# Weights in one flat DRAM tensor in load order, and modulation on TensorE with four row tiles per load

## The chip, the cores and the metric

The kernel runs on one core of a Trainium2 chip. A core has a matrix engine (TensorE, PE in the profile; PEld is its weight load), VectorE (DVE), ScalarE (ACT), GpSimd (POOL) and a sync engine (SP) that issues the DMA transfers here. The metric is the device time of one execution in microseconds, lower is better; several runs are taken and the median counts. One of the executions is profiled, and all rows below come from it.

## The reference

One layer of an encoder over 256 tokens of width 2048, batch 1, all in float32. A conditioning vector c gives a shift, a scale and a gate for each of two sub-layers (adaLN modulation); one input projection feeds eight retention heads and eight latent-attention (MLA) heads; an output projection, a SwiGLU and a final norm follow.

```python
c_act = silu(c)
mod = (c_act @ ada_w + ada_b)                     # 2048 -> 6 x 2048
shift_a, scale_a, gate_a, shift_f, scale_f, gate_f = split(mod, 6)
h = rmsnorm(x, norm1_w) * (1 + scale_a) + shift_a
proj = h @ w_in                                   # 2048 -> 5184
q_r, k_r, v_r, g_r, cq, ckv, k_rope = split(proj)
ret_out = silu(g_r) * groupnorm(retention(rope(q_r), rope(k_r), v_r))
q_m = rmsnorm(cq) @ w_uq;  kv = rmsnorm(ckv) @ w_ukv
mla_out = rmsnorm(softmax_attention(q_m, kv, rope(k_rope)))
x = x + gate_a * (concat(ret_out, mla_out) @ w_o)
h = rmsnorm(x, norm2_w) * (1 + scale_f) + shift_f
x = x + gate_f * ((silu(h @ w_gate) * (h @ w_up)) @ w_down)     # 2048 -> 5632 -> 2048
return rmsnorm(x, final_norm_w)
```

Weights are read once: some 312 MB in one execution, a third of it ada_w.

## The kernel before

Weights arrive in loads of mostly 512 KB into one of six staging buffers `stg` (128 partitions of 1024 floats). A load of a projection weight covers two row tiles of 128 rows and 512 columns: in the DRAM matrix that is, per partition, two pieces of 2 KB, one from each row tile. `split_weights` (line 97) issues it from SP (line 101), ACT rounds it to `whi` (line 103), DVE makes the remainder `wlo` (line 105), each with three buffers. PE multiplies in three products, activation-high by whi, activation-high by wlo, activation-low by whi (lines 111 to 113), in one-pass float32r, for two token blocks; a load of 512 columns thus feeds 12 matmuls.

The modulation is a matrix-vector product. `ada_set` (line 153) makes it for one of six sections and `nk` column tiles of 128, so `n` = 128 nk columns, from loads of `kk` row tiles (line 155: two where nk is 4, four where it is 2). A set goes to DVE or to PE, by strings of 0 and 1 (lines 41, 43, 55) and, for the first gate_f set, a fixed choice. On DVE each row tile is one multiply-add into `ada_acc` (line 179). On PE each row tile is one plain float32 matmul (line 175) with 32 columns of stationary operand (`c_pad`, one of them not zero) and the n weight columns streaming. Row tile k goes to partitions 32 (k mod 4) of a PSUM bank, that is to one of four column strips of 32 columns of the array:

```python
q = 32 * (k % 4)
PE.matmul(a[q:q + 32, 0:n], lhsT=c_pad[:, k], rhs=w[:, j], start=k < 4, stop=k >= KT - 4)
```

`finish` and `spread` then sum the strips and bring the result into `mod`, `gate_a` or `gate_f`.

There are ten sets on PE: two of 256 columns at the start, one more of 256 columns at about 200 us, and seven of 512 columns, eight loads each.

The order of the program is a list of steps. `run` (line 131) walks it and starts the loads of later steps as long as at most LOOK = 3 are ahead and it does not stand at a step of URGENT. `ada_stream` cuts the modulation into units of one load, which are spread among the projection steps, so that PE, DVE and the DMA queue are all used. A scheduler then sets each engine's final order. Each engine works through its own order, and waits there for semaphores; a load can be issued when the last reader of its buffer, mostly DVE, is done.

In time: the first modulation and the norm of x (to 26 us), the input projection in four groups of row tiles with the next group's modulation between (to some 240 us), the latent projections and attention, the retention heads with the output projection and gate_a, shift_f and scale_f (to 533 us), SwiGLU and down projection (to the end).

Of the kernel before, what the change touches and what calls it, by code (L numbers as in the profile page):

```python
# [8 lines left out]
F32 = mybir.dt.float32  # L9
# [47 lines left out]
URGENT = ("finish", "spread", "build_h2", "build_h1")  # L57
# [3 lines left out]

@with_exitstack
def encoder_block(ctx: ExitStack, tc: tile.TileContext, x, cols, rows, pos, ada_w, w_in, w_uq, w_ukv, w_o,
                  w_gate, w_up, w_down, out):
# [64 lines left out]
    # ---- steps: ("w", source, body) takes split weights, ("a", load, body) a loaded tile, ("f", body, name) nothing;  # L129
    # no loads are started ahead at the URGENT ones ----  # L130
# [175 lines left out]
    def project(gi, name, c0, widths):  # L306
# [3 lines left out]
        def body(kp, whi, wlo):  # L310
# [22 lines left out]
            ("w", w_in[(k0 + kp) * P:(k0 + min(kp + 2, nk)) * P, c0:c0 + sum(widths)], lambda hi, lo, kp=kp: body(kp, hi, lo))  # L333
# [92 lines left out]
    def up_q(hf):  # L426
# [31 lines left out]
        ws = [("w", w_uq[k * P:(k + 1) * P, hf * 768:(hf + 1) * 768], lambda hi, lo, k=k: body(k, hi, lo)) for k in range(4)]  # L458
# [511 lines left out]
```

## Time and profile before

| | before |
|---|---|
| median of 3 runs | 1287.1 us |
| lowest and highest | 1284.15 and 1289.62 us |
| span of the profiled execution | 1284.4 us |
| PE busy | 1241.4 us (97%) |
| DVE busy | 844.6 us (66%) |
| ACT busy | 599.6 us (47%) |
| DMA queue, share of 16 engines | 75.1% |
| HBM read | 312.11 MB, mean rate 245 GB/s with the writes |

The profile gives no time of the profiled execution but its span, from the first to the last instruction; it lies inside the range of the three runs, 2.7 us under their median. A row of a view in order of time gives start, duration, engine, line, operation, the tile written and the tiles read. Matmuls are pipelined, so how long PE needs for one is read from start to start, not from its duration. DMA share is the part of the time in which the 16 DMA engines have a packet under way; it can exceed 1 where packets overlap.

### The profile page before, as it was taken

How to read it: one execution, taken by the hardware profiler on the slowest of the kernel's cores; microseconds unless marked ns; L12 is line 12 of the kernel's file. 1: busy time of each engine (PE TensorE's matmuls, PEld its weight loads, DVE VectorE, ACT ScalarE, POOL GpSimd, SP SyncE). 2: the span in 40 equal slices, each digit the busy share in tenths (PEclk: the TensorE clock that was granted, in tenths of full speed). 3: DMA queues.
4: the chain of work that ended last, by engine and by line, in shares of the span. 5: the costliest groups of instructions: out<-in, count | busy, mean ns of one | idle time of the engine just before them, and what ended most of it. 6: DMA issues, size and time to landing. Idle time of an engine off the chain costs nothing.

```text
span 1284.4 us, 15784 instructions
## 1 busy us (share of the span) xinstructions
PE 1241.4 (97%) x5798; PEld 967.1 (75%) x5798; DVE 844.6 (66%) x1185; ACT 599.6 (47%) x811; POOL 1.7 (0%) x9
## 2 busy tenths in 40 slices
PE   5999999999999999899999999999999999999997
PEld 1576657678776688578888888888888888888885
DVE  2596788779997699797556546554754454545544
ACT  3553445555546565556444344444444443434443
POOL 0000000000000000000000000000000000000000
PEclk8999999999999999999999999999999999999999
DMA  9898898887887789798777767775876655565562
GB/s 315 304 298 297 263 315 290 291 293 255 303 258 262 264 290 316 255 336 299 217 225 217 225 191 252 233 213 167 279 230 198 221 189 192 196 196 193 190 193 97
DMA packets 166621, 315.24 MB, mean 245 GB/s; under 512 B 10248, under 2 KB 22664, under 8 KB 166032
## 3 DMA queue, kind: packets, MB, share of 16 engines
q1 hardware_dynamic: 166544, 314.24, 75.1%
q8 instruction: 45, 0.74, 0.2%
q14 instruction: 32, 0.26, 0.1%
HBM read 312.11 MB, written 2.10 MB: 245 GB/s over the span
## 4 chain that ended last, share of the span: by engine, by line
PE 82%; DVE 8%; DMA 5%; ACT 2%; issue 2%; SPq 0%; ACTq 0%; DVEq 0%
PE bank L112 24%; PE bank L113 24%; PE bank L111 23%; PE bank L175 4%; DVE wlo L105 3%; DVE ada_acc L179 2%; PE bank L127 2%; DMA stg<-in_ada_w 2%; DMA stg<-in_w_in 1%; DMA stg<-in_w_o 1%; ACT whi L103 1%; PE bank L491 1%; PE bank L490 1%; PE bank L515 1%; PE bank L592 1%
## 5 line engine op out<-in xcount | busy, mean ns | idle before, releaser
L105 DVE TENSOR_TENSOR wlo<-stg,whi 128x1024 fp32r<-128x1024 f32 (+2 forms) x400 | 478.7, 1199 | 343.4 <-ACT whi L103 336.5
L103 ACT CAST whi<-stg 128x1024 fp32r<-128x1024 f32 (+2 forms) x400 | 412.7, 1033 | 534.2 <-PE bank L113 418.6
L111 PE MATMUL bank<-whi,actt 128*128 128x512 f32 (+1 forms) x1184 | 457.4, 392 | 9.9 <-ACT whi L103 6.4
L112 PE MATMUL bank<-wlo,actt 128*128 128x512 f32 (+1 forms) x1184 | 460.2, 389 | 6.9 <-DVE wlo L105 6.1
L113 PE MATMUL bank<-whi,actt 128*128 128x512 f32 (+1 forms) x1184 | 457.9, 387 | 0.7 <-DVE actt L124 0.7
L111 PEld LDWEIGHTS bank<-whi,actt 128*128 128x128 f32 x1184 | 221.7, 188 | 69.5 <-ACT whi L103 13.1
L112 PEld LDWEIGHTS bank<-wlo,actt 128*128 128x128 f32 x1184 | 223.3, 189 | 63.6 <-DVE wlo L105 16.3
L113 PEld LDWEIGHTS bank<-whi,actt 128*128 128x128 f32 x1184 | 222.9, 188 | 45.2 <-DVE actt L124 1.4
L179 DVE SCALAR_TENSOR_TENSOR ada_acc<-stg,c_act,ada_acc 128x512 f32<-128x512 f32 (+1 forms) x240 | 175.0, 730 | 18.0 <-DMA stg<-in_ada_w 15.0
L111 PE MATMUL bank<-whi,ap 128*128 128x512 f32 x352 | 137.0, 389 | 0.0
L113 PE MATMUL bank<-whi,ap 128*128 128x512 f32 x352 | 136.9, 389 | 0.0
L112 PE MATMUL bank<-wlo,ap 128*128 128x512 f32 x352 | 136.9, 389 | 0.0
L175 PE MATMUL bank<-stg,c_pad 128*32 128x512 f32 (+1 forms) x320 | 67.3, 584 | 14.7 <-DMA stg<-in_ada_w 14.7
L111 PEld LDWEIGHTS bank<-whi,ap 128*128 128x128 f32 x352 | 66.1, 188 | 13.8
L113 PEld LDWEIGHTS bank<-whi,ap 128*128 128x128 f32 x352 | 66.1, 188 | 13.8
L112 PEld LDWEIGHTS bank<-wlo,ap 128*128 128x128 f32 x352 | 66.1, 188 | 13.5
L175 PEld LDWEIGHTS bank<-stg,c_pad 128*32 128x32 f32 x320 | 10.2, 114 | 38.3 <-issue 27.3
L205 DVE TENSOR_REDUCE mod<-bank 128x4 f32<-128x512 f32 (+3 forms) x18 | 8.0, 443 | 15.6 <-PE bank L201 15.6
L829 ACT ACTIVATE sgs<-bank 128x512 f32<-128x512 f32 x22 | 13.1, 597 | 10.5 <-PE bank L113 9.9
L124 DVE TENSOR_TENSOR actt<-hfull,actt 128x256 fp32r<-128x256 f32 x40 | 16.3, 418 | 1.3 <-ACT actt L123 1.3
L831 DVE TENSOR_TENSOR sgs<-bank,sgs 128x512 f32<-128x512 f32 x22 | 14.3, 682 | 0.6 <-PE bank L113 0.6
L811 DVE TENSOR_TENSOR ap<-bank,ap 128x512 fp32r<-128x512 f32 x22 | 14.1, 681 | 0.0
(222 smaller groups left out, 712.3 us busy)
## 6 DMA issues: line engine op xcount, KB each, us to landing
stg<-in_ada_w SPq DMA_DIRECT2D x192, 512.0 KB, 5.1
stg<-in_w_gate SPq DMA_DIRECT2D x88, 512.0 KB, 4.7
stg<-in_w_up SPq DMA_DIRECT2D x88, 512.0 KB, 4.2
stg<-in_w_down SPq DMA_DIRECT2D x88, 512.0 KB, 3.6
stg<-in_w_in SPq DMA_DIRECT2D x72, 512.0 KB, 4.7
stg<-in_w_o SPq DMA_DIRECT2D x32, 512.0 KB, 4.9
stg<-in_w_in SPq DMA_DIRECT2D x16, 288.0 KB, 3.8
stg<-in_w_ukv SPq DMA_DIRECT2D x8, 512.0 KB
```

Source lines behind the costliest of these rows:

```text
L103: S.copy(hi, stg)
L105: V.tensor_tensor(lo, stg, hi.bitcast(F32), op=ALU.subtract)
L111: PE.matmul(o, lhsT=ah, rhs=whi, start=first, stop=False)
L112: PE.matmul(o, lhsT=ah, rhs=wlo, start=False, stop=False)
L113: PE.matmul(o, lhsT=al, rhs=whi, start=False, stop=last)
L124: V.tensor_tensor(dst[:, k, T:2 * T], tmp, dst[:, k, 0:T].bitcast(F32), op=ALU.subtract)
L127: PE.transpose(b[:, j, tb * P:(tb + 1) * P], src, ident)
L175: PE.matmul(a[q:q + 32, 0:n], lhsT=c_pad[:, k], rhs=w[:, j], start=k < 4, stop=k >= KT - 4)
L179: V.scalar_tensor_tensor(out=a, in0=w[:, j], scalar=c_act[:, k:k + 1], in1=a, op0=ALU.mult, op1=ALU.add)
L811: V.tensor_tensor(ap[:, ks, T:2 * T], b, ap[:, ks, 0:T].bitcast(F32), op=ALU.subtract)
L829: S.activation(sg, o[tb], AF.Silu)
L831: V.tensor_tensor(sg, o[tb], sg, op=ALU.mult)
```

## The change

The host packs all weight matrices into one flat tensor `stream`. The kernel takes blocks from it in the order in which the loads are written (`Stream.take`), and notes for each block which rows and columns of which matrix it holds; `Stream.pack` fills the tensor by these notes. A block is laid out partition by partition, so that a load of kt row tiles and n columns reads kt x n floats in one piece per partition: 4 KB for most, 2304 bytes for the narrow w_in loads, 3 KB for w_uq as before. The bytes, the number of loads and the buffers are as before.

In a set on PE, a load now covers at most 256 columns (`wide`) and as many row tiles as fill 4 KB (`kk = 1024 // wide`). For the 512-column sets that is four row tiles of one half of the columns, where it was two row tiles of all columns; the loads go through all row tiles of the left half and then of the right half. Sets on DVE, and sets of 256 columns, keep their shape.

```diff
+class Stream:
+    def __init__(self, ap):
+        self.ap, self.at, self.plan = ap, 0, []
+
+    def take(self, name, k0, kt, c0, n):
+        self.plan.append((name, k0, kt, c0, n))
+        a = self.at
+        self.at += P * kt * n
+        return self.ap[a:self.at].rearrange("(p f) -> p f", p=P)
+
+    def pack(self, np, weights):
+        flat = np.empty(self.at, np.float32)
+        a = 0
+        for name, k0, kt, c0, n in self.plan:
+            b = weights[name][k0 * P:(k0 + kt) * P, c0:c0 + n].reshape(kt, P, n).transpose(1, 0, 2)
+            flat[a:a + b.size] = b.reshape(-1)
+            a += b.size
+        return flat
...
     def split_weights(src):
-        k, n = src.shape
-        kt = k // P
+        _, _, kt, _, n = src
         stg = wp.tile([P, kt * n], F32, name="stg", tag="stg", bufs=6)
-        SY.dma_start(stg.rearrange("p (k n) -> p k n", k=kt), src.rearrange("(k p) n -> p k n", p=P))
+        SY.dma_start(stg, stream.take(*src))
...
     def ada_set(pool, sec, k0, nk, rowdst, on_pe):
         n = nk * P
-        kk = {1: 8, 2: 4, 3: 2, 4: 2}[nk]
+        wide = n if not on_pe else min(n, 2 * P)
+        kk = 1024 // wide
...
-        def load(t):
-            w = wp.tile([P, kk, n], F32, name="stg", tag="stg", bufs=6)
-            c0 = sec * D + k0 * P
-            SY.dma_start(w, ada_w[t * kk * P:(t + 1) * kk * P, c0:c0 + n].rearrange("(k p) n -> p k n", p=P))
+        def load(c, t):
+            w = wp.tile([P, kk, wide], F32, name="stg", tag="stg", bufs=6)
+            SY.dma_start(w.rearrange("p k n -> p (k n)"), stream.take("ada_w", t * kk, kk, sec * D + k0 * P + c, wide))
             return w
 
-        def body(t, w):
-            if t == 0:
+        def body(c, t, w):
+            if c == 0 and t == 0:
                 acc["t"] = bank() if on_pe else acc_tile()
...
-                    PE.matmul(a[q:q + 32, 0:n], lhsT=c_pad[:, k], rhs=w[:, j], start=k < 4, stop=k >= KT - 4)
+                    PE.matmul(a[q:q + 32, c:c + wide], lhsT=c_pad[:, k], rhs=w[:, j], start=c == 0 and k < 4, stop=c + wide == n and k >= KT - 4)
...
-        loads = [("a", lambda t=t: load(t), lambda w, t=t: body(t, w)) for t in range(KT // kk)]
+        loads = [
+            ("a", lambda c=c, t=t: load(c, t), lambda w, c=c, t=t: body(c, t, w)) for c in range(0, n, wide) for t in range(KT // kk)
+        ]
...
-            ("w", w_in[(k0 + kp) * P:(k0 + min(kp + 2, nk)) * P, c0:c0 + sum(widths)], lambda hi, lo, kp=kp: body(kp, hi, lo))
+            ("w", ("w_in", k0 + kp, min(2, nk - kp), c0, sum(widths)), lambda hi, lo, kp=kp: body(kp, hi, lo))
```

The other weights (w_uq, w_ukv, w_o, w_gate, w_up, w_down) are named in the same way as w_in. The scheduler makes a new order for each engine. On PE, in the second group of the input projection (`actt` is the activation, `bank` a PSUM bank, `c_pad` the conditioning vector), before:

```order
285 L112 MATMUL bank<-wlo,actt 128x512
286 L113 MATMUL bank<-whi,actt 128x512
287 L175 MATMUL bank<-stg,c_pad 32x512 x2
288 L111 MATMUL bank<-whi,actt 128x512
289 L112 MATMUL bank<-wlo,actt 128x512
```

and after, where line numbers are 21 higher:

```order
286 L133 MATMUL bank<-wlo,actt 128x512
287 L134 MATMUL bank<-whi,actt 128x512
288 L196 MATMUL bank<-stg,c_pad 32x256 x4
289 L132 MATMUL bank<-whi,actt 128x512
290 L133 MATMUL bank<-wlo,actt 128x512
```

A load's two matmuls of 512 columns are four of 256 at the same place. On PE in the retention stage (L592 and L603, later L615 and L626, are the scores and the outputs of a retention head, L201 the transposes of a finished modulation set), before:

```order
1466 L113 MATMUL bank<-whi,actt 128x512
1467 L175 MATMUL bank<-stg,c_pad 32x512 x2
1468 L592 MATMUL bank<-qT,kT 128x256 x2
1469 L175 MATMUL bank<-stg,c_pad 32x512 x2
1470 L603 MATMUL bank<-acc_v,rP 128x128 x4
1471 L111 MATMUL bank<-whi,actt 128x512 x2
1472 L175 MATMUL bank<-stg,c_pad 32x512 x2
1473 L201 MATMUL bank<-ident,ada_acc 128x128 x3
```

and after:

```order
1464 L134 MATMUL bank<-whi,actt 128x512
1465 L196 MATMUL bank<-stg,c_pad 32x256 x4
1466 L615 MATMUL bank<-qT,kT 128x256 x2
1467 L196 MATMUL bank<-stg,c_pad 32x256 x4
1468 L626 MATMUL bank<-acc_v,rP 128x128 x4
1469 L132 MATMUL bank<-whi,actt 128x512 x2
1470 L133 MATMUL bank<-wlo,actt 128x512
1471 L134 MATMUL bank<-whi,actt 128x512
```

The loads stand at the same places; the third one here has moved further back. On ACT, in the first group of the input projection (`xnT` is the transposed x, `acc_cq` and `acc_ck` sums of the projection), before:

```order
14 L327 COPY acc_cq<-bank 128x512 x2
15 L103 CAST whi<-stg 128x576
16 L253 COPY xnT<-bank 128x512
17 L327 COPY acc_ck<-bank 128x288 x2
18 L253 COPY xnT<-bank 128x512
```

and after:

```order
14 L350 COPY acc_cq<-bank 128x512 x2
15 L276 COPY xnT<-bank 128x512
16 L124 CAST whi<-stg 128x576
17 L350 COPY acc_ck<-bank 128x288 x2
18 L276 COPY xnT<-bank 128x512
```

The copy of xnT and the cast have changed places.

## Rows read from the trace of the kernel before

**Rows 1.** The page, parts 1 and 4: busy time and share, chain by engine.
```profile
PE 1241.4 (97%) x5798; PEld 967.1 (75%) x5798; DVE 844.6 (66%) x1185; ACT 599.6 (47%) x811; POOL 1.7 (0%) x9
PE 82%; DVE 8%; DMA 5%; ACT 2%; issue 2%; SPq 0%; ACTq 0%; DVEq 0%
```

**Rows 2.** Stretches: length, busy (count) of PE, PEld, DVE, ACT, POOL, PEclk, DMA share, GB/s.
```profile
0.00:600.00 600.00, 565.73 (x2781) 408.40 (x2782) 471.49 (x816) 311.25 (x499) 1.72 (x9) 0.99 0.87 291
600.00:1284.00 684.00, 675.71 (x3019) 558.73 (x3017) 373.08 (x369) 288.38 (x313) 0.00 (x0) 1.00 0.66 205
...
50.00:100.00 50.00, 44.25 (x211) 34.46 (x209) 45.68 (x66) 28.15 (x41) 0.00 (x0) 1.00 0.93 313
100.00:150.00 50.00, 49.30 (x211) 33.11 (x212) 34.47 (x48) 18.85 (x24) 0.00 (x0) 1.00 0.86 279
150.00:200.00 50.00, 45.60 (x223) 29.66 (x221) 42.78 (x97) 23.43 (x30) 0.00 (x0) 1.00 0.93 310
240.00:300.00 60.00, 60.00 (x305) 40.94 (x304) 45.56 (x94) 30.14 (x54) 0.00 (x0) 1.00 0.83 274
400.00:450.00 50.00, 50.00 (x243) 30.39 (x243) 35.39 (x84) 30.14 (x55) 0.00 (x0) 1.00 0.84 281
540.00:600.00 60.00, 59.16 (x249) 45.99 (x249) 52.96 (x72) 35.69 (x49) 0.00 (x0) 0.97 0.95 329
```

**Rows 3.** PE in order of time, one modulation load of 512 columns.
```profile
104.71 0.39 PE L112 MATMUL bank<-wlo,actt 128*128 128x512 f32 x1
104.94 0.39 PE L113 MATMUL bank<-whi,actt 128*128 128x512 f32 x1
105.26 1.05 PE L175 MATMUL bank<-stg,c_pad 128*32 128x512 f32 x4
106.24 0.50 PE L111 MATMUL bank<-whi,actt 128*128 128x512 f32 x1
```

**Rows 4.** PE in order of time, two loads of 512 columns in one run.
```profile
174.29 1.06 PE L175 MATMUL bank<-stg,c_pad 128*32 128x512 f32 x8
175.29 0.73 PE L111 MATMUL bank<-whi,actt 128*128 128x512 f32 x2
```

**Rows 5.** PE in order of time, one and four matmuls of 256 columns.
```profile
203.14 0.62 PE L175 MATMUL bank<-stg,c_pad 128*32 128x256 f32 x2
203.69 0.50 PE L112 MATMUL bank<-wlo,actt 128*128 128x512 f32 x1
...
209.86 0.64 PE L175 MATMUL bank<-stg,c_pad 128*32 128x256 f32 x8
210.43 0.73 PE L111 MATMUL bank<-whi,actt 128*128 128x512 f32 x2
```

**Rows 6.** Groups by line and shape, count, busy, mean ns, idle before: line 175.
```profile
L175 PE MATMUL bank<-stg,c_pad 128*32 128x512 f32 x224 | 56.1, 608 | 1.1 <-DMA stg<-in_ada_w 1.1
```

**Rows 7.** PE in order of time, the gate_f set before the SwiGLU.
```profile
526.92 1.92 PE L175 MATMUL bank<-stg,c_pad 128*32 128x512 f32 x16
528.77 0.44 PE L127 MATMUL bank<-ident,x 128*128 128x128 f32 x2
...
536.86 0.73 PE L111 MATMUL bank<-whi,actt 128*128 128x512 f32 x2 [2.60 <-ACT whi L103]
```

**Rows 8.** Busy time by stretch: the load of x, and the first modulation loads.
```profile
3.00:9.00 6.00, 0.00 (x0) 0.00 (x0) 0.41 (x2) 2.00 (x2) 0.00 (x0) 1.00 0.98 388
10.00:22.00 12.00, 8.48 (x66) 1.89 (x66) 3.30 (x7) 3.39 (x5) 0.00 (x0) 1.00 1.09 355
```

**Rows 9.** Waits of PE from 25 to 600 us: total, times, longest.
```profile
PE bank L111 <- ACT whi L103: 6.4, 6, 2.6
PE bank L112 <- DVE wlo L105: 6.1, 11, 1.4
```

**Rows 10.** PE in order of time: the first modulation loads.
```profile
12.56 1.08 PE L175 MATMUL bank<-stg,c_pad 128*32 128x256 f32 x8 [0.33 <-DMA stg<-in_ada_w]
14.07 1.08 PE L175 MATMUL bank<-stg,c_pad 128*32 128x256 f32 x8 [0.42 <-DMA stg<-in_ada_w]
```

More of the change, by code (lines that the diff above doesn't have):

```diff
@@ L59, with encoder_block @@
 DVE_DELAY = 2
+class Stream:
[14 more added lines that the diff above has]
+        return flat
 @with_exitstack
-def encoder_block(ctx: ExitStack, tc: tile.TileContext, x, cols, rows, pos, ada_w, w_in, w_uq, w_ukv, w_o,
-                  w_gate, w_up, w_down, out):
+def encoder_block(ctx: ExitStack, tc: tile.TileContext, x, cols, rows, pos, stream, out):
     nc = tc.nc
@@ L456, in turned @@
             S.copy(qrT[:, hf * 2:hf * 2 + 2], tr)
-        ws = [("w", w_uq[k * P:(k + 1) * P, hf * 768:(hf + 1) * 768], lambda hi, lo, k=k: body(k, hi, lo)) for k in range(4)]
+        ws = [("w", ("w_uq", k, 1, hf * 768, 768), lambda hi, lo, k=k: body(k, hi, lo)) for k in range(4)]
         return ws + [f(roll)], [f(turned)]
@@ L478, in body @@
                     S.copy(m["v"][:, tb, hf * 512:(hf + 1) * 512], st["v"][tb])
-        return [("w", w_ukv[k * P:(k + 1) * P, hf * 1024:(hf + 1) * 1024], lambda hi, lo, k=k: body(k, hi, lo)) for k in range(4)]
+        return [("w", ("w_ukv", k, 1, hf * 1024, 1024), lambda hi, lo, k=k: body(k, hi, lo)) for k in range(4)]
     scale_m = 192.0 ** -0.5
@@ L681, in body @@
                 st["w"] = []
-            return [("w", w_o[k * P:(k + 2) * P, cs], lambda hi, lo, k=k: body(k, hi, lo)) for k in range(k0, k0 + 8, 2)]
+            return [("w", ("w_o", k, 2, n * CH, CH), lambda hi, lo, k=k: body(k, hi, lo)) for k in range(k0, k0 + 8, 2)]
         return [chunk(n) for n in range(4)]
@@ L831, in body @@
                     V.tensor_tensor(sg, o[tb], sg, op=ALU.mult)
-        cs = slice(j * CH, (j + 1) * CH)
-        return [("w", w[kp * P:(kp + 2) * P, cs], lambda hi, lo, kp=kp: body(kp, hi, lo)) for kp in range(0, KT, 2)]
+        return [("w", (w, kp, 2, j * CH, CH), lambda hi, lo, kp=kp: body(kp, hi, lo)) for kp in range(0, KT, 2)]
     units = ada_stream(None, [(GT_F, 4 * i, 4, lambda: late["gate_f"], False) for i in range(N_FILL, 4)])
     n_ch = DFF // CH
-    g0, u0, g1, u1 = [gate_up(j, n, w) for j in range(2) for n, w in (("g", w_gate), ("u", w_up))]
+    g0, u0, g1, u1 = [gate_up(j, n, w) for j in range(2) for n, w in (("g", "w_gate"), ("u", "w_up"))]
     h_late = [(sec, K_LATE, KT - K_LATE, None) for sec in (SC_F, SH_F) if K_LATE < KT]
@@ L860, in encoder_block @@
     for j in range(1, n_ch):
-        ws = u1 if j == 1 else gate_up(j, "g", w_gate) + gate_up(j, "u", w_up)
+        ws = u1 if j == 1 else gate_up(j, "g", "w_gate") + gate_up(j, "u", "w_up")
         for i, w in enumerate(ws):
@@ L906, in body @@
             st["w"] = []
-        return [("w", w_down[kp * P:(kp + 2) * P, cs], lambda hi, lo, kp=kp: body(kp, hi, lo)) for kp in range(0, FT, 2)]
+        return [("w", ("w_down", kp, 2, n * CH, CH), lambda hi, lo, kp=kp: body(kp, hi, lo)) for kp in range(0, FT, 2)]
     def finish(tb):
@@ L956 @@
     ])[None, :]
-    arrays = {
-        "x": a["x"][0], "cols": cols, "rows": rows, "pos": a["positions"][0].reshape(NB, P).T,
-        "ada_w": a["ada_w"][0], "w_in": a["w_in"][0], "w_uq": a["w_uq"][0], "w_ukv": a["w_ukv"][0], "w_o": a["w_o"][0],
-        "w_gate": a["w_gate"][0], "w_up": a["w_up"][0], "w_down": a["w_down"][0],
-    }
+    weights = {n: a[n][0] for n in ("ada_w", "w_in", "w_uq", "w_ukv", "w_o", "w_gate", "w_up", "w_down")}
+    arrays = {"x": a["x"][0], "cols": cols, "rows": rows, "pos": a["positions"][0].reshape(NB, P).T}
     arrays = {k: np.ascontiguousarray(v) for k, v in arrays.items()}
@@ L964 @@
     aps = [nc.dram_tensor(f"in_{k}", v.shape, mybir.dt.from_np(v.dtype), kind="ExternalInput").ap() for k, v in arrays.items()]
+    total = sum(w.size for w in weights.values())
+    stream = Stream(nc.dram_tensor("in_stream", (total,), F32, kind="ExternalInput").ap())
     o = nc.dram_tensor("out", (T, D), F32, kind="ExternalOutput").ap()
     with tile.TileContext(nc) as tc:
-        encoder_block(tc, *aps, o)
+        encoder_block(tc, *aps, stream, o)
+    assert stream.at == total
+    arrays["stream"] = stream.pack(np, weights)
     r = run_bass_kernel_spmd(nc, [{f"in_{k}": v for k, v in arrays.items()}], core_ids=[0])
```

## The prediction

> **What bounds the kernel now.** I read the page first. TensorE (PE) is busy 97% of the span, and 82% of the chain of work that ended last lies on it [rows 1]. So an edit counts if it takes time from PE or from what PE waits for. The busy time by stretch comes next [rows 2]. From 600 us to the end PE is busy 676 of 684 us with the DMA queue at a share of 0.66: the SwiGLU and down projections wait for no load, and a quicker load is worth nothing there. In the first 600 us PE is idle 34.3 us and the queue's share is 0.87, so both could matter there.
>
> The third view is the order of time on PE around the modulation matmuls, line 175. The trace holds two records for each of these f32 matmuls (x4 is two). In the input projection, L113 starts at 104.94, the two 512-wide matmuls of a load at 105.26, the next L111 at 106.24 [rows 3]. That is 1.30 us where neighbours without modulation start 0.23 apart (104.71 and 104.94). A load on PE therefore costs 1.07 us of PE. Three of its parts do not depend on how many matmuls it holds: 0.32 us to get in, the streaming of 512 columns, and a tail. Two such loads run back to back, on four column strips, take 174.29 to 175.29 without the entry, 1.00 us, where the single one takes 105.26 to 106.24, 0.98 [rows 3, 4]: strips run side by side, and one load of two row tiles leaves two of the four idle.
>
> The kernel already holds the new form, in the sets that are 256 columns wide: four matmuls of 256 columns go from 209.86 to the next L111 at 210.43, in 0.57 us, and one alone from 203.14 to 203.69, in 0.55 [rows 5]. That is the template for what the change does to the others.
>
> **Part 1, the column strips.** The 512-wide form has 224 records [rows 6]: 112 matmuls of 512 columns in 56 loads, which become 224 of 256 columns in 56 loads. A load then carries four row tiles for the four strips. What counts is how they stand in runs on PE, since a run pays entry and tail once. The order of instructions gives, before, 9 runs of one, 33 of two, 3 of three, 5 of four and 1 of eight; after, without the 256-wide sets that were there before, 5 of one, 2 of three, 35 of four, 2 of seven, 4 of eight, one of 11 and one of 16.
>
> Net prices (the neighbours' 0.23 taken off): a run of one to four at 512 columns 1.06 to 1.09 us [rows 3, 4]. The run of eight, two rounds of four strips, lasts from 526.92 to 528.77, 1.85 us, against 1.00 for the single round at 174.29 [rows 4, 7]; so a second round adds 0.85 and the run costs 1.94 net. At 256 columns, one matmul costs 0.32 + 0.55 - 0.23 = 0.64, four 0.32 + 0.57 - 0.23 = 0.66 [rows 5], and each further round half of 0.85, 0.43: 1.09 for seven or eight, 1.52 for 11, 1.95 for 16. Before: 9 x 1.06 + 33 x 1.07 + 3 x 1.08 + 5 x 1.09 + 1.94 = 55.5 us. After: 5 x 0.64 + 2 x 0.65 + 35 x 0.66 + 6 x 1.09 + 1.52 + 1.95 = 37.6 us.
>
> By place: 1.7 us in the first projection group (28 to 49 us), 3.3 in the second (105 to 137), 2.1 in the third (160 to 185), 4.8 around the latent up-projections (241 to 275), 5.8 in the retention stage (398 to 447). The set at 527 us gives nothing: its runs of 16 and 11 cost what 8 and 3 cost, and its last run ends into a wait of 2.60 us for ACT at 536.86 [rows 7]. Sum **-17.7 us**.
>
> What is late next is the loads. The same bytes must arrive in less time. Stretch by stretch [rows 2], rate times old length over new: 100 to 150 us, 279 becomes 299 GB/s; 150 to 200, 310 becomes 324; 240 to 300, 274 becomes 298; 400 to 450, 281 becomes 318. The highest rates that long stretches reached are 329 (540 to 600, PE nearly never idle) and 310 to 313, where PE was idle 4 to 6 us of 50. So the third group gives back its 2.1 us, and the retention stage a third of 5.8: **+4.0 us**. The ends are 0 and 13 (the third rival).
>
> **Part 2, the weights as one flat tensor.** A load of 512 KB now reads one contiguous 4 KB piece per partition, instead of two of 2 KB (four of 1 KB in the 256-wide sets, two of 1152 B in the narrow w_in loads). Same bytes, same number of loads, same buffers. No row shows such a load from a flat tensor. GB/s over the queue's share [rows 2, 8] bounds it: 355/1.09 = 326 where 1 KB pieces run, 313/0.93 = 337 and 329/0.95 = 346 with 2 KB, 388/0.98 = 396 with the 8 KB pieces of x. I take 360 for 4 KB, nearer the 2 KB rows than the 8 KB row: 6% over 340, or 1.46 us instead of 1.54 per load. Some 97 loads lie in the stretches with a share of 0.93 and more (160 us at about 317 GB/s), so the queue gains 8 us; PE's waits behind loads from 25 to 600 us are 6.4 + 6.1 = 12.5 us [rows 9]. I take a third of them, **-4.2 us**; the ends are 0 and 12.5.
>
> At the start PE takes one load of 1 KB pieces each 1.51 us (12.56 to 14.07) and waits for DMA before it [rows 10], 347 GB/s. At the 388 of x [rows 8] it would be 1.35, eight times 0.16 = 1.3 us. I take **-1.0**, ends 0 and 1.3.
>
> **The order.** ACT and DVE rows change places here and there, as in the first ACT rows shown, where a copy of xnT now goes ahead of a cast. The scheduler's shuffles have no sign that I can read; PE's longest wait for ACT or DVE after 25 us is 2.6 us [rows 9], so one such wait more or less is the bound. I take 0, ends -2.6 and +2.6. SP issues as many loads as before, and PE's waits are as many.
>
> **The sum.** 1284.4 - 17.7 + 4.0 - 4.2 - 1.0 = 1265.5 us of span. The median of the runs, 1287.1, is 2.7 above the span of the profiled one, so **1268 us**.
>
> **Rivals.**
> Pieces of 2 KB are as good as 4 KB. The 1 KB and 2 KB rows lie close (326, 337, 346); against it stands the 396 of x [rows 8]. Then the terms -4.2 and -1.0 fall away: 1284.4 - 13.7 + 2.7 = 1273. The Trainium skill, "DMA: Bandwidth & Descriptors", section Specifications, has 512 B as the smallest transfer for line rate, by which 1 KB pieces would already be as quick as 8 KB. The trace does not agree: 326 against 396.
>
> Quicker loads than I think: if 4 KB pieces run like x, PE's 12.5 us behind loads go, nothing is given back, and the start gains 1.3: 1284.4 - 17.7 - 12.5 - 1.3 + 2.7 = 1256. Against it: DVE is busy 45.7 of 50 us from 50 to 100 [rows 2], and part of those waits is its own.
>
> The loads take back the time. If the queue gives no more than now, PE's gain from 100 to 200 us and in the retention stage becomes waits for whi and wlo, and half of that around the up-projections too: 1.7 + 2.4 = 4.1 kept, 1283. For it: the shares of 0.84 to 0.93. Against it: 329 GB/s at 540.
>
> Slower. The contiguous block makes the 16 DMA engines read addresses 4 KB apart where they read rows of different pitch; if they then collide in memory, the first 600 us, 291 GB/s x 600 us = 175 MB [rows 2], become DMA-bound. The queue's full rate is now 291/0.87 = 334. It decides below 288, where the 175 MB take 606 us and more. At 280 they take 624, +24 us: 1284.4 + 24 + 2.7 = 1311. Nothing in the rows speaks for it but that no flat load was measured.
>
> **How the numbers follow.** My forecast, strips mostly kept and loads a little quicker: 0.65, with its own range of 1262 to 1276. Equal pieces 0.12, quick loads 0.08, gain taken back 0.10, slower 0.05. A measurement of this kernel tells about 0.5% (6.4 us) from no change, so faster means below 1280.7. Forecast, equal pieces and quick loads are faster: 0.85. Taken back is within: 0.10. Slower 0.05. The range of 1253 to 1279 holds the first three and leaves out the last two.
>
> **What would show it.** Right: four modulation matmuls (x8 in the trace) between L113 and the next projection matmul in about 0.89 us, entry included; PE busy time down by some 18 us, all of it before 450 us; the SwiGLU and down stage still about 684 us long; first loads less than 1.5 us apart; higher GB/s at the same share. Wrong: 1.1 us and more for the four would mean that strips don't run side by side out of one load; PE idle from 100 to 450 us up by 10 us would mean that the loads took it; a full rate under 300 GB/s would mean that the flat layout is bad. What would make the prediction wrong is above all the size of the load term, which rests on a rate between two rows.

## The result and the profile after

The changed kernel takes 1266.0 us (median of 4 runs, 1262.57 to 1266.85) where the kernel before takes 1287.9 (4 runs, 1284.15 to 1289.62): a ratio of 0.983, with an interval of 0.980 to 0.985. 1268 was predicted, with a range of 1253 to 1279. The profiled execution's span is 1264.9 us, where the sum gave 1265.5.

In the changed file the lines of the helpers stand 21 further down: the modulation matmul is L196 (before L175), the three projection matmuls are L132, L133, L134 (before L111 to L113), the casts that make whi and wlo are L124 and L126, and a load of projection weights is issued in L122.

The page of the changed kernel, parts 1, 3 and 4: busy time by engine, the queue, and the chain that ended last. It answers to [rows 1].

```profile
PE 1224.4 (97%) x6022; PEld 971.6 (77%) x6022; DVE 843.6 (67%) x1185; ACT 599.7 (47%) x811; POOL 1.7 (0%) x9
...
q1 hardware_dynamic: 88720, 314.24, 72.0%
...
PE 85%; DVE 5%; DMA 5%; ACT 2%; issue 1%; SPq 0%; ACTq 0%; DVEq 0%
```

PE has lost 17.0 us of busy time (1241.4 to 1224.4), and the span 19.5. So most of the gain is time in which PE used to work. It is still busy 97% of the span, and its share of the chain has grown.

The stretches of the changed kernel, with the columns of [rows 2]: length, busy time and count of PE, PEld, DVE, ACT and POOL, granted clock, DMA share, GB/s.

```profile
0.00:600.00 600.00, 568.70 (x3097) 429.52 (x3098) 481.90 (x828) 321.24 (x511) 1.71 (x9) 0.99 0.85 299
600.00:1264.00 664.00, 655.70 (x2927) 542.07 (x2925) 361.71 (x358) 278.43 (x301) 0.00 (x0) 1.00 0.61 205
...
100.00:150.00 50.00, 47.97 (x269) 35.34 (x268) 36.17 (x55) 20.39 (x27) 0.00 (x0) 1.00 0.87 288
150.00:200.00 50.00, 46.66 (x243) 30.35 (x244) 40.58 (x90) 22.00 (x27) 0.00 (x0) 0.97 0.90 313
240.00:300.00 60.00, 60.00 (x361) 45.32 (x360) 50.09 (x91) 34.26 (x67) 0.00 (x0) 1.00 0.84 290
400.00:450.00 50.00, 50.00 (x294) 38.19 (x291) 44.82 (x95) 32.30 (x56) 0.00 (x0) 1.00 0.86 309
```

From 100 to 150 us, from 240 to 300 and from 400 to 450 the queue moves 288, 290 and 309 GB/s, where before it moved 279, 274 and 281, and its share has hardly risen [rows 2]. The quicker PE does ask for more, and gets it.

Where the time went shows when the two traces are laid beside each other at the same projection matmul, counted from the first in order of time. The table is worked out from the start times in the traces. Each column is that kernel's start of the n-th projection matmul less the start in the kernel before; the w_uq and w_ukv projections, which have lines of their own, are counted too. "Strips alone" and "flat alone" are the first two experiments below.

| n-th projection matmul (its start before) | changed | strips alone | flat alone |
|---|---|---|---|
| first (25.6 us) | -2.6 | +0.4 | -2.7 |
| 240 (96 us) | -4.2 | -0.8 | -2.2 |
| 500 (170 us) | -8.0 | -4.9 | -2.0 |
| 600 (203 us) | -7.2 | -3.4 | -2.0 |
| 900 (273 us) | -11.0 | -7.8 | -2.5 |
| 1300 (386 us) | -12.8 | -8.4 | -3.7 |
| 1400 (436 us) | -17.4 | -12.1 | -3.7 |
| 1700 (520 us) | -20.0 | -14.6 | -4.7 |
| from 600 us on | -20.0 | -13.8 | -4.5 |

The gain comes in at five places: the start, the second projection group, the latent up-projections, the retention stage, and its end. Between 170 and 203 us some of it is given back. From 600 us to the end the difference stays what it is: the SwiGLU and the down projection take as long as before.

Now the load itself. PE of the changed kernel in order of time, one load, which answers to [rows 3], and a run of two loads. The count behind L196 is twice its matmuls, as before.

```profile
100.72 0.39 PE L134 MATMUL bank<-whi,actt 128*128 128x512 f32 x1
101.04 0.64 PE L196 MATMUL bank<-stg,c_pad 128*32 128x256 f32 x8
101.61 0.50 PE L132 MATMUL bank<-whi,actt 128*128 128x512 f32 x1
...
167.78 0.40 PE L134 MATMUL bank<-whi,actt 128*128 128x512 f32 x1
168.11 1.07 PE L196 MATMUL bank<-stg,c_pad 128*32 128x256 f32 x16
169.11 0.73 PE L132 MATMUL bank<-whi,actt 128*128 128x512 f32 x2
```

From L134 to the next L132 the load takes 101.61 - 100.72 = 0.89 us, where 512 columns on two strips took 1.30. Two rounds take 1.33.

PE's waits from 25 to 600 us in the changed kernel (total, times, longest), against 6.4 and 6.1 us in [rows 9]:

```profile
PE bank L132 <- ACT whi L124: 8.4, 6, 2.7
PE bank L133 <- DVE wlo L126: 7.0, 14, 1.1
```

These waits have risen from 12.5 to 15.4 us. The prediction let the flat layout take a third of them away.

### The profile page after: what moved, and what is told of

It is laid out like the page before. It is cut to its first block, busy times and chain, and to the rows that moved or that the text cites. A ratio compares the mean times of both kernels' runs of the same rounds, so it can differ in the third digit from the quotient of the medians.

```text
span 1264.9 us, 16232 instructions
## 1 busy us (share of the span) xinstructions
PE 1224.4 (97%) x6022; PEld 971.6 (77%) x6022; DVE 843.6 (67%) x1185; ACT 599.7 (47%) x811; POOL 1.7 (0%) x9
## 3 DMA queue, kind: packets, MB, share of 16 engines
q1 hardware_dynamic: 88720, 314.24, 72.0%
## 4 chain that ended last, share of the span: by engine, by line
PE 85%; DVE 5%; DMA 5%; ACT 2%; issue 1%; SPq 0%; ACTq 0%; DVEq 0%
PE bank L133 25%; PE bank L134 25%; PE bank L132 25%; DMA stg<-in_stream 5%; DVE wlo L126 2%; PE bank L148 2%; PE bank L196 2%; DVE ada_acc L200 1%; ACT whi L124 1%; PE bank L514 1%; PE bank L138 1%; PE bank L513 1%; PE bank L626 1%; PE bank L615 1%; PE bank L140 1%
## 5 line engine op out<-in xcount | busy, mean ns | idle before, releaser
L126 DVE TENSOR_TENSOR wlo<-stg,whi 128x1024 fp32r<-128x1024 f32 (+2 forms) x400 | 478.7, 1198 | 341.2 <-ACT whi L124 339.6
L124 ACT CAST whi<-stg 128x1024 fp32r<-128x1024 f32 (+2 forms) x400 | 412.8, 1033 | 532.3 <-PE bank L134 417.2
L132 PE MATMUL bank<-whi,actt 128*128 128x512 f32 (+1 forms) x1184 | 457.9, 393 | 11.7 <-ACT whi L124 8.4
L133 PE MATMUL bank<-wlo,actt 128*128 128x512 f32 (+1 forms) x1184 | 461.7, 390 | 7.4 <-DVE wlo L126 7.0
L134 PE MATMUL bank<-whi,actt 128*128 128x512 f32 (+1 forms) x1184 | 459.2, 388 | 0.3 <-DVE actt L145 0.3
L132 PEld LDWEIGHTS bank<-whi,actt 128*128 128x128 f32 x1184 | 222.0, 189 | 64.9 <-ACT whi L124 12.7
L133 PEld LDWEIGHTS bank<-wlo,actt 128*128 128x128 f32 x1184 | 223.7, 189 | 62.4 <-DVE wlo L126 17.0
L134 PEld LDWEIGHTS bank<-whi,actt 128*128 128x128 f32 x1184 | 223.7, 189 | 44.9 <-DVE actt L145 1.1
L200 DVE SCALAR_TENSOR_TENSOR ada_acc<-stg,c_act,ada_acc 128x512 f32<-128x512 f32 (+1 forms) x240 | 175.0, 730 | 15.8 <-DMA stg<-in_stream 12.8
L132 PE MATMUL bank<-whi,ap 128*128 128x512 f32 x352 | 137.0, 389 | 0.0
L134 PE MATMUL bank<-whi,ap 128*128 128x512 f32 x352 | 136.9, 389 | 0.0
L133 PE MATMUL bank<-wlo,ap 128*128 128x512 f32 x352 | 136.9, 389 | 0.0
L133 PEld LDWEIGHTS bank<-wlo,ap 128*128 128x128 f32 x352 | 66.1, 188 | 13.8
L132 PEld LDWEIGHTS bank<-whi,ap 128*128 128x128 f32 x352 | 66.1, 188 | 13.8
L134 PEld LDWEIGHTS bank<-whi,ap 128*128 128x128 f32 x352 | 66.1, 188 | 13.5
L196 PE MATMUL bank<-stg,c_pad 128*32 128x256 f32 x544 | 48.0, 415 | 11.1 <-DMA stg<-in_stream 11.0
L196 PEld LDWEIGHTS bank<-stg,c_pad 128*32 128x32 f32 x544 | 13.0, 112 | 35.2 <-issue 26.0
L834 DVE TENSOR_TENSOR ap<-bank,ap 128x512 fp32r<-128x512 f32 x22 | 14.1, 681 | 0.0
```

The lines of the kernel that those rows point to most:

```text
L124: S.copy(hi, stg)
L126: V.tensor_tensor(lo, stg, hi.bitcast(F32), op=ALU.subtract)
L132: PE.matmul(o, lhsT=ah, rhs=whi, start=first, stop=False)
L133: PE.matmul(o, lhsT=ah, rhs=wlo, start=False, stop=False)
L134: PE.matmul(o, lhsT=al, rhs=whi, start=False, stop=last)
L196: PE.matmul(a[q:q + 32, c:c + wide], lhsT=c_pad[:, k], rhs=w[:, j], start=c == 0 and k < 4, stop=c + wide == n and k >= KT - 4)
```

## The experiments

Each of the ten kernels was compared with the kernel before on the same chip. Ratios are to that kernel; edits are against the changed kernel unless it says otherwise.

### Each part by itself

Strips alone: the kernel before, with its weights in matrices, and the first half of the change (the loop over the halves is as in the change).

```diff
-        kk = {1: 8, 2: 4, 3: 2, 4: 2}[nk]
+        wide = n if not on_pe else min(n, 2 * P)
+        kk = 1024 // wide
...
-            w = wp.tile([P, kk, n], F32, name="stg", tag="stg", bufs=6)
-            c0 = sec * D + k0 * P
-            SY.dma_start(w, ada_w[t * kk * P:(t + 1) * kk * P, c0:c0 + n].rearrange("(k p) n -> p k n", p=P))
+            w = wp.tile([P, kk, wide], F32, name="stg", tag="stg", bufs=6)
+            c0 = sec * D + k0 * P + c
+            SY.dma_start(w, ada_w[t * kk * P:(t + 1) * kk * P, c0:c0 + wide].rearrange("(k p) n -> p k n", p=P))
...
-                    PE.matmul(a[q:q + 32, 0:n], lhsT=c_pad[:, k], rhs=w[:, j], start=k < 4, stop=k >= KT - 4)
+                    PE.matmul(a[q:q + 32, c:c + wide], lhsT=c_pad[:, k], rhs=w[:, j], start=c == 0 and k < 4, stop=c + wide == n and k >= KT - 4)
```

> The four-strip loads alone; the weights stay in their matrices, so a modulation load on PE reads four pieces of 1 KB per partition and the projection loads two of 2 KB as before. My theory (PE time falls by 17.7 us, the loads give 4.0 of it back, the flat layout was a gain of its own): 13.7 us under the kernel before, about 1274. Rival A, the layout brings nothing and the strips all: the time of the changed kernel, 1266. Rival B, without quicker loads PE only waits more: within 5 us of the kernel before, 1283 to 1288, with PE's waits for ACT and DVE up by about 13 us.

Measured: 1272.1 us, ratio 0.989 (0.986 to 0.991), 15.2 us less than before. The profiled spans differ by 1284.4 - 1270.6 = 13.8, and 13.7 was predicted for the strips with what the loads give back.

Flat alone: the changed kernel with the loads on PE as wide as they were.

```diff
-        wide = n if not on_pe else min(n, 2 * P)
+        wide = n
```

> The flat tensor alone; loads of two row tiles by 512 columns on PE as before. My theory (quicker loads shorten PE's waits by 4.2 us and the start by 1.0): about 1282.7. Rival A, the layout brings nothing: 1288. Rival B, the start gains about 2.6 us as in the trace of the changed kernel and the waits gain nothing: about 1285.

Measured: 1283.0 us, ratio 0.997 (0.995 to 0.999). The spans differ by 4.0, where 5.2 was predicted. PE's waits of strips alone, from 25 to 600 us, and then those of flat alone:

```profile
PE bank L111 <- ACT whi L103: 9.6, 6, 3.1
PE bank L112 <- DVE wlo L105: 6.3, 13, 0.8
```
```profile
PE bank L133 <- DVE wlo L126: 6.3, 11, 1.1
PE bank L132 <- ACT whi L124: 6.3, 5, 3.2
```

The strips alone raise the waits from 12.5 us to 15.9, by 3.4: that is what they give back, and 4.0 was predicted. The flat layout alone leaves them at 12.6. So what it gains, it doesn't gain there. The table says where: 2.7 of its 4.5 us are there before the first projection matmul.

### What in the flat layout is quicker

The flat tensor with each block stored row tile by row tile: a load is still one contiguous block of DRAM, but in pieces of 2 KB for the projections and 1 KB for the modulation on PE (`pack` and `split_weights` are changed to match).

```diff
-        return self.ap[a:self.at].rearrange("(p f) -> p f", p=P)
+        return self.ap[a:self.at].rearrange("(k p f) -> p k f", p=P, k=kt)
...
-            SY.dma_start(w.rearrange("p k n -> p (k n)"), stream.take("ada_w", t * kk, kk, sec * D + k0 * P + c, wide))
+            SY.dma_start(w, stream.take("ada_w", t * kk, kk, sec * D + k0 * P + c, wide))
```

> The changed kernel with each block still contiguous in the flat tensor, but stored row tile by row tile, so that a load reads two pieces of 2 KB per partition (four of 1 KB on PE's modulation sets). It tells the size of the pieces from the contiguity of the block. If the size of the pieces makes the loads quicker: like the strips alone, about 1274. If contiguity does: like the changed kernel, 1266.

Beside it the changed kernel ran once more:

> The changed kernel once more, beside the three others on the same chip: 1266, ratio 0.983. All theories expect the same; it is the mark the others are held against.

Measured: 1268.4 us, ratio 0.985 (0.982 to 0.987), and for the changed kernel 1265.1, 0.982 (0.980 to 0.985). The small pieces lie between the two expectations. Their interval overlaps that of strips alone and that of the changed kernel, though all six runs (1264.68 to 1270.13) lie under all six of strips alone (1270.62 to 1275.85). The start can be told apart. The stretch of 10 to 20 us, in which PE takes one modulation load after the other, in the changed kernel and in the one with small pieces:

```profile
10.00:20.00 10.00, 8.68 (x66) 1.93 (x66) 3.30 (x7) 2.79 (x6) 0.00 (x0) 1.00 1.03 413
```
```profile
10.00:20.00 10.00, 7.55 (x58) 1.73 (x58) 3.30 (x7) 2.77 (x5) 0.00 (x0) 1.00 1.10 349
```

Here small pieces, of 1 KB, run at 349/1.10 = 317 GB/s of a full queue, and 4 KB pieces at 413/1.03 = 401. Strips alone, with 1 KB pieces out of rows, have 350/1.10 = 318. At the start it is the size of the pieces alone. Over the whole span both count. The page gives the queue's packets, its MB and its share; of strips alone, and then of small pieces:

```profile
q1 hardware_dynamic: 180880, 314.24, 75.7%
```
```profile
q1 hardware_dynamic: 180880, 314.24, 73.9%
```

The MB over share times span is the mean rate of a full queue. It is 314.24/(0.757 x 1270.6) = 327 GB/s for strips alone, 336 for small pieces with as many packets, and 345 in the changed kernel with half of them (342 in its second run). So of some 5%, about half comes with the contiguous block, and half with the longer pieces. They come at different places. From 610 to 1240 us, in the SwiGLU and the down projection, all pieces are of 2 KB in strips alone and in small pieces, and of 4 KB in the changed kernel:

```profile
610.00:1240.00 630.00, 630.00 (x2815) 521.24 (x2814) 345.65 (x335) 266.21 (x283) 0.00 (x0) 1.00 0.66 210
```
```profile
610.00:1240.00 630.00, 630.00 (x2814) 521.12 (x2813) 345.33 (x335) 266.78 (x284) 0.00 (x0) 1.00 0.63 210
```
```profile
610.00:1240.00 630.00, 630.00 (x2815) 521.12 (x2814) 345.39 (x334) 266.78 (x284) 0.00 (x0) 1.00 0.63 210
```

For the same 210 GB/s the queue needs a share of 0.66 with 2 KB rows, and 0.63 with a contiguous block, in pieces of 2 KB or of 4 KB (0.64 in the changed kernel's second run). There it is the contiguous block, and the longer pieces add nothing. In the first 600 us the small pieces move 298 GB/s at a share of 0.88, strips alone 296 at 0.89, and the changed kernel 299 at 0.85: there it is mostly the length, and mostly that of the 1 KB pieces. Sixteen times a packet's bytes over its mean time, worked out from the packets in the traces from 30 to 600 us, is 324 GB/s for the 1 KB packets and 346 for the 2 KB packets of the small pieces, and 354 for the 4 KB packets of the changed kernel (353 in its second run).

### What the loads still cost

The changed kernel with half of the bytes in each modulation load. The matmuls and DVE operations are as many as before; the DVE lines are changed as the matmul line is.

```diff
-            SY.dma_start(w.rearrange("p k n -> p (k n)"), stream.take("ada_w", t * kk, kk, sec * D + k0 * P + c, wide))
+            src = stream.take("ada_w", t * kk, kk, sec * D + k0 * P + c, wide)
+            SY.dma_start(w[:, 0:kk // 2].rearrange("p k n -> p (k n)"), src[:, 0:kk * wide // 2])
...
-                    PE.matmul(a[q:q + 32, c:c + wide], lhsT=c_pad[:, k], rhs=w[:, j], ...
+                    PE.matmul(a[q:q + 32, c:c + wide], lhsT=c_pad[:, k], rhs=w[:, j % (kk // 2)], ...
```

> The changed kernel, but every modulation load brings only the first half of its row tiles (256 KB instead of 512), and the matmuls and multiply-adds use that half twice; the modulation values are therefore not the reference's. Instructions and loads are as many as before, the bytes of the first 600 us fall by about a quarter. My theory (what PE still waits for after 25 us is the arrival of loads): the 15.4 us of waits for ACT and DVE fall to a third or less, time about 1254, start about 5 us earlier included in that: 1250. Rival (these waits belong to DVE, ACT and the order of the program): the waits stay within 3 us of 15.4, and the time falls by the start alone, to about 1261.

Measured: 1253.5 us, ratio 0.974 (0.970 to 0.979). Its first 600 us, PE's waits from 25 to 600 us (the list's first four rows; whi is in it no more), and the page's busy times:

```profile
0.00:600.00 600.00, 572.41 (x3160) 440.60 (x3161) 489.92 (x839) 326.09 (x516) 1.72 (x9) 0.99 0.71 229
```
```profile
PE bank L132 <- ACT actt L144: 5.8, 3, 2.1
PE bank L223 <- DVE ada_acc L201: 3.3, 2, 2.0
PE bank L148 <- DVE rout L321: 1.5, 1, 1.5
PE bank L133 <- DVE wlo L126: 1.3, 3, 0.6
```
```profile
PE 1214.0 (97%) x6022; PEld 970.8 (78%) x6022; DVE 841.8 (67%) x1185; ACT 598.9 (48%) x811; POOL 1.7 (0%) x9
```

The waits for whi and wlo fall from 15.4 us to 1.3, while DVE and ACT have as much to do as before. So these waits are the arrival of loads, and not the length of ACT's or DVE's own work. That the span falls by as much (1264.9 - 1250.8 = 14.1) does not mean that they make the difference. PE's other waits from 25 to 600 us rise from 1.8 us to some 12, and its busy time falls by 1224.4 - 1214.0 = 10.4; only 3.7 of the 14.1 us are idle time of PE. Of the 10.4, the modulation matmuls make 4.6 (48.0 us to 43.4), and a granted clock of 0.996 over the span, where it was 0.992, is part of the rest. The engines' order is another one too. So what the 15.4 us of waits would give by themselves is not shown.

One more load started ahead, with the same six buffers:

```diff
-LOOK = 3
+LOOK = 4
```

> The changed kernel with LOOK = 4 instead of 3: one more load may be under way before its step; six staging buffers as before. If loads arrive late because they are issued late: PE's waits after 25 us fall from 15.4 to below 10 and the time to about 1260. If buffers, not the limit, hold the issue: the same time, 1264 to 1268.

Measured: 1266.6 us, ratio 0.984 (0.981 to 0.988). PE's waits from 25 to 600 us, and then what SP's queue waits for most, first in the changed kernel and then with LOOK at 4:

```profile
PE bank L132 <- ACT whi L124: 8.5, 7, 3.8
PE bank L133 <- DVE wlo L126: 5.1, 12, 0.8
```
```profile
SPq L122 <- DVE wlo L126: 540.1, 279, 4.0
```
```profile
SPq L122 <- DVE wlo L126: 529.0, 277, 4.4
```

Nothing is gained. The issue of a load waits for DVE to be done with a staging buffer, with either number. A seventh buffer was not tried.

### What makes a load of four cheap

The changed kernel with all four matmuls of a load on the same strip: `q` goes by the load and not by the matmul.

```diff
-                    q = 32 * (k % 4)
-                    PE.matmul(..., start=c == 0 and k < 4, stop=c + wide == n and k >= KT - 4)
+                    q = 32 * (k // 4)
+                    PE.matmul(..., start=c == 0 and k % 4 == 0, stop=c + wide == n and k % 4 == 3)
```

> The changed kernel with one edit: row tile k goes to column strip k // 4 instead of k % 4, so the four matmuls of a load lie on the same strip. Loads, bytes and matmul counts are the same. My theory (the gain of the new loads is that four strips stream at once): four times two passes of 0.21 us instead of one time two, 1.28 us more for each of 56 + 4 loads at full clock, about 75 us slower than the changed kernel, 1340. Rival (the gain is in fewer entries and tails of loads, and not in the strips): within 10 us of the changed kernel, 1266 to 1276.

Measured: 1335.4 us, ratio 1.038 (1.033 to 1.043). PE in order of time, a load between projection matmuls:

```profile
115.17 0.39 PE L134 MATMUL bank<-whi,actt 128*128 128x512 f32 x1
115.48 1.91 PE L196 MATMUL bank<-stg,c_pad 128*32 128x256 f32 x8
117.33 0.50 PE L132 MATMUL bank<-whi,actt 128*128 128x512 f32 x1
```

117.33 - 115.17 = 2.16 us, where the changed kernel takes 0.89. The matmuls, their number, the bytes and the loads are the same; only the strip differs. The group of these matmuls (count, busy, mean ns, idle before) in the changed kernel and in this one:

```profile
L196 PE MATMUL bank<-stg,c_pad 128*32 128x256 f32 x544 | 48.0, 415 | 11.1 <-DMA stg<-in_stream 11.0
```
```profile
L196 PE MATMUL bank<-stg,c_pad 128*32 128x256 f32 x544 | 118.1, 393 | 10.7 <-DMA stg<-in_stream 10.7
```

PE is busy 118.1 - 48.0 = 70.1 us longer with them, and the span is 1332.5 - 1264.9 = 67.6 us longer. The prediction took the sets that were 256 columns wide as the template; without strips side by side nothing of part 1 is left: this kernel is slower than the one before.

The same load as eight matmuls of 128 columns in place of four of 256:

```diff
-        wide = n if not on_pe else min(n, 2 * P)
+        wide = n if not on_pe else min(n, P)
```

> The changed kernel with loads of eight row tiles by 128 columns on PE: per load twice the matmuls at half the width, the same bytes and the same streamed columns. My theory (a load costs entry, streamed columns and tail, and the number of matmuls next to nothing): within 3 us of the changed kernel, 1264 to 1269. Rival (each further matmul costs by itself, some 60 cycles, 25 ns, for each pass): 4 matmuls x 2 passes x 25 ns x 68 loads = 14 us more, 1280.

Measured: 1263.7 us, ratio 0.983 (0.980 to 0.986), the same as the changed kernel.

```profile
99.19 0.39 PE L134 MATMUL bank<-whi,actt 128*128 128x512 f32 x1
99.50 0.64 PE L196 MATMUL bank<-stg,c_pad 128*32 128x128 f32 x16
100.08 0.50 PE L132 MATMUL bank<-whi,actt 128*128 128x512 f32 x1
```

100.08 - 99.19 = 0.89 us, for twice as many matmuls. The price hangs on the columns that each strip streams, not on how many matmuls bring them. The Trainium skill, "TensorEngine Tiling (Array Packing)", section Instruction Overhead, gives each matmul an overhead of some 60 cycles. The trace shows nothing of it between 8 and 16 records, neither of which is as short as 60 columns.

### Work moved onto PE and off it

One more modulation set on PE instead of DVE, at the new price:

```diff
-ADA_PE = "10010100101101"
+ADA_PE = "11010100101101"
```

> The changed kernel with one more modulation set moved from DVE to PE (shift_a of row tiles 2 to 5, worked on from about 50 to 80 us, where DVE is busy 45.7 of 50 us). PE then spends eight times 0.66 = 5.3 us more, DVE 12 us less. If DVE holds that stretch: PE's waits there (5 us) go, and the time is about the same, 1264 to 1268. If loads hold it: the 5.3 us are added, 1271.

Measured: 1265.1 us, ratio 0.983 (0.980 to 0.987), the changed kernel's time. DVE's busy time from 50 to 100 us falls from 45.71 us to 36.28, and PE's waits for whi and wlo from 15.4 to 5.0 + 4.9 = 9.9:

```profile
50.00:100.00 50.00, 47.40 (x254) 36.12 (x250) 36.28 (x51) 25.82 (x38) 0.00 (x0) 1.00 0.90 308
```

The waits are 5.5 us shorter, with as many loads and bytes: part of what makes loads late is DVE's work. That it frees the buffers sooner when it has less to do is the likely way, but was not followed up. PE spends 52.6 us with the modulation matmuls where it was 48.0. Its busy time as a whole is 1224.6 us, where the changed kernel's is 1224.4; the granted clock over the span is 0.995 where it was 0.992, so that the time stays the same is in part the clock.

And that kernel without the gate_f set that PE does just before the SwiGLU. The prediction gave that set nothing, since PE waits right behind it; this puts it to the test.

```diff
-N_FILL = 1
+N_FILL = 0
```

> The kernel with one more early set on PE (e8), and the gate_f set that stands on PE before the SwiGLU (at 507 us in the changed kernel) moved to DVE in the SwiGLU stage, where DVE is busy 362 of 655 us. My theory (its PE time before the SwiGLU lies in the wait for the second norm and gives nothing, but eight loads fewer stand ahead of the first SwiGLU weights): 1 to 3 us under the changed kernel, 1262 to 1265. Rival (PE's 4.8 us there are on the path): 1260. Rival (without it PE idles, and DVE's load work delays wlo in the SwiGLU): 1266 to 1272.

Measured: 1273.5 us, ratio 0.990 (0.988 to 0.992), some 8 us over its sibling: a miss. The longest of PE's waits from 25 to 600 us, and then its only one from 1000 to 1100 us:

```profile
PE bank L148 <- DVE x L687: 5.4, 1, 5.4
```
```profile
PE bank L218 <- DVE ada_acc L212: 5.6, 1, 5.6
```

Projection matmul by projection matmul, the two kernels are up to 2.4 us apart in the first 334 us, but within 0.1 us of each other from there to 497 us, just before the set, and within 0.2 from 583 to 956. So the set's place gives no time, as predicted: without its matmuls PE waits 5.4 us for DVE instead. How much of that is the wait and how much a slower clock (0.89 granted from 480 to 540 us, where the sibling has 0.94) is open. But the set's loads don't vanish. They join the gate_f sets that DVE does beside the SwiGLU (225 of its 512-wide multiply-adds, where the sibling has 210), and these now end later: from 1012.6 us PE waits 5.6 us for DVE's sum. At the end of this wait the granted clock falls to its lower level (1.2 GHz); it is 0.93 in this stretch, where its sibling has 1.00:

```profile
1000.00:1050.00 50.00, 44.40 (x185) 35.58 (x184) 30.02 (x33) 16.41 (x18) 0.00 (x0) 0.93 0.73 256
```

By the clock 0.07 x 50 = 3.5 us are lost, an estimate; with the wait that is 9.1 of the 9.8 us by which the spans differ (1271.8 and 1262.0). The expectation had only the place from which the work was taken, and not the one where it would land.

## Why the prediction was right

**What bounds the kernel.** PE, as read. The busy time that PE lost (17.0 us, 18 predicted) makes up most of what the span lost (19.5), and the part after 600 us has not moved.

**The price of a load.** 0.89 us with its entry was predicted from the 256-wide sets in [rows 5], and 0.89 was measured. The second round, predicted at half of [rows 7], came to 1.33 us in all, against 0.23 + 1.09 = 1.32. That strips run side by side was read from [rows 3, 4] and is shown by the kernel with one strip for each load.

**Where it counts.** By place the prediction had 1.7 us by 49 us, 3.3 in the second group, 4.8 at the up-projections, 5.8 in the retention stage and none at 527 us. Strips alone give 1.2 between the first matmul and the 240th, 4.1 from there to the 500th, 4.4 from the 600th to the 900th, and 3.7 + 2.5 between the 1300th and the 1700th. The gate_f set gives nothing that lasts; it ends in a wait for ACT of 2.68 us, where before it was 2.60 [rows 7]:

```profile
506.93 1.93 PE L196 MATMUL bank<-stg,c_pad 128*32 128x256 f32 x32
508.79 0.44 PE L148 MATMUL bank<-ident,x 128*128 128x128 f32 x2
...
516.01 0.73 PE L132 MATMUL bank<-whi,actt 128*128 128x512 f32 x2 [2.68 <-ACT whi L124]
```

The set starts 526.92 - 506.93 = 20.0 us earlier, and the next projection matmul 536.86 - 516.01 = 20.9; by 600 us it is 20.0 again. That its run of 11 costs what 3 cost was misread, by the prediction's own prices (1.52 and 1.08), but it has no weight in the sum.

**What the loads take back.** 4.0 us was predicted, 2.1 of it in the third projection group and 1.9 in the retention stage. Strips alone raise the waits by 3.4. From 150 to 200 us they go from 3.0 us before to 5.2, as predicted. In the retention stage there is 0.2; the rest stands behind it, from 450 to 600 us (3.9 before, 4.9 with strips alone). The sum was right, one of the two places was not.

In the third group the waits are not all of it; the prediction had no term for the clock. In strips alone a wait of 2.95 us for whi ends at 154.4 us, and behind it the granted clock is at the lower of its two levels (1.2 of 2.4 GHz) for some 3.4 us. The changed kernel has the same behind a wait of 2.56 us, in the second run of 2.61 (0.97 from 150 to 200 us in both). The kernel before has 1.00 there [rows 2]. The small pieces, with the same strips and 4.7 us of waits from 150 to 200 us, wait 2.40 us at that place and stay at 1.00. Strips alone in that stretch, and then the small pieces:

```profile
154.70:157.90 3.20, 3.06 (x7) 1.96 (x7) 3.20 (x7) 0.43 (x1) 0.00 (x0) 0.50 0.95 301
```
```profile
150.00:200.00 50.00, 45.17 (x247) 30.05 (x247) 41.37 (x94) 22.81 (x29) 0.00 (x0) 1.00 0.98 323
```

From the 400th projection matmul (144 us) to the 600th, strips alone lose 0.7 us against the kernel before, and the small pieces gain 1.8. The slow clock takes half of 3.4 us, 1.7, by estimate. So that this group's 2.1 us were all given back is the clock as well as the loads.

**The flat layout: the rate.** 6% over 340 GB/s was taken for 4 KB pieces, between the 2 KB rows and x. The mean of a full queue rose from 314.24/(0.751 x 1284.4) = 326 to 345, by 5.9% (flat alone 339, by 4.2). The size of that term was right. Its reason, 4 KB pieces in place of 2 KB, was right in part only: at equal layout 4 KB packets were 2% quicker than 2 KB in the first 600 us (354 against 346 GB/s), and from 610 us on the share was 0.63 with either. The rest is the contiguous block, which the prediction did not set apart.

**The flat layout: what it is worth.** Here two terms were mis-sized, in opposite directions. "I take a third of them, -4.2 us" did not come: flat alone leaves PE's waits at 12.6 us, and in the changed kernel they are 15.4, only 0.5 less than with strips alone (14.8 in its second run). In its place the start gave more than "-1.0": 2.7 with flat alone and 2.6 with the change, beyond the end of 1.3 that was put to it. PE of the changed kernel, three of the first modulation loads, as in [rows 10]:

```profile
12.61 1.08 PE L196 MATMUL bank<-stg,c_pad 128*32 128x256 f32 x8 [0.20 <-DMA stg<-in_stream]
13.90 1.08 PE L196 MATMUL bank<-stg,c_pad 128*32 128x256 f32 x8 [0.21 <-DMA stg<-in_stream]
15.18 1.08 PE L196 MATMUL bank<-stg,c_pad 128*32 128x256 f32 x8 [0.20 <-DMA stg<-in_stream]
```

The loads are 1.29 us apart, not 1.51, and 1.35 was the best that the prediction allowed, from the rate of x. The first load also starts 1.0 us earlier (10.14 us, 11.16 before), though 0.5 of that is there with strips alone too. Start and waits together were to give 5.2; flat alone gave 4.0, and the change 1284.4 - 1264.9 - 13.8 = 5.7 beyond strips alone. Behind the start the change gains 3.2 us on strips alone, where flat alone gains 1.8 on the kernel before; of the 3.2, 0.5 is in the waits for whi and wlo and 2.1 in PE's other waits, mostly for DVE. The sum came out because the two errors nearly cancel: that is luck.

Why a quicker queue did not shorten the waits is in part shown. They are the arrival of loads, as half the bytes show, and starting loads earlier by one doesn't help, since the issue stands at the buffers. A set taken off DVE shortens them by 5.5 us. That a load which flies 5% shorter saves PE little, because the time until its buffer is free is most of what it waits, was only argued.

**The rivals.** Pieces of 2 KB as good as 4 KB (1273): its time did not come, but its premise nearly holds: from 610 to 1240 us both need a share of 0.63, and before 600 us packets of 2 KB run at 346 and of 4 KB at 354 GB/s. It left out the contiguous block and the pieces of 1 KB: at the start these run at 317 and 4 KB at 401 GB/s. The section Specifications of "DMA: Bandwidth & Descriptors" in the Trainium skill would have them equal from 512 B on, and the trace differs. Quick loads (1256): the rate of x was reached at the start alone, and the waits for whi and wlo did not go. Half of the modulation bytes came there, 1253, but not by the waits alone. Gain taken back (1283): the waits took 3.4, not 13. Slower: the flat blocks run at a higher rate, not a lower one.

**The order.** It was taken as 0, with ends at 2.6 either way. As far as the names and shapes of tiles in the traces tell, flat alone runs PE, DVE and ACT in the order of the kernel before, and small pieces and the changed kernel in the order of strips alone. So what the new order is worth is part of the 13.8 us of strips alone, and no run shows it by itself. The parts alone make 13.8 + 4.0 = 17.8 us of span, together 19.5, and 1.7 us of it can't be given a cause; the order isn't one. Two runs of the changed kernel differ by 0.9 (1264.9 and 1264.0).

## What to carry to other kernels

A matmul with few rows should get loads that fill all the strips: count the columns which each strip streams, with the entry and the end once for each run, and look for that form elsewhere in the same trace before you build it. A quicker transfer is worth its full gain only where the engine takes one load after the other; where the issue stands at a buffer, price it by taking bytes away and not by the rate, and split what comes of it into waits and busy time before you call it the waits' price. A wait that ends in a slower clock costs more than its length. And when work is taken from one place, follow it to where it lands, to the last unit of its queue.

## What the runs showed of the hardware

- The number of f32 matmuls in a load makes no difference here: 8 and 16 records both take 0.89 us, at 256 and 128 columns.
- 4 KB pieces reached 401 GB/s of a full queue at the start, no less than the 8 KB pieces of x at 388/0.98 = 396 [rows 8].
- With as many packets (180,880), contiguous blocks came to 336 GB/s of a full queue over the span where rows of a matrix came to 327, though at the start, with 1 KB pieces, contiguity alone gave nothing (317 and 318). From 610 to 1240 us a contiguous block of 2 KB pieces needed the share of one of 4 KB pieces, 0.63 for 210 GB/s, and 2 KB rows 0.66.
- In three runs the granted clock was at its lower level (1.2 of 2.4 GHz) for some 3.4 us right behind PE's longest wait between 150 and 200 us (2.56 to 2.95 us).
